# Recurrent stage of a hybrid attention, RWKV-7 and Mamba-2 kernel: Gram products over 64 rows in two row groups, and copies in place of transposes around the triangular inverse

## The chip, the cores and the metric

One Trainium2 chip, one core of it. The kernel is one program on the five engines of that core: TensorE (PE in the profile, with its weight loads apart as PEld), VectorE (DVE), ScalarE (ACT), GpSimd (POOL) and SyncE (SP), which issues DMAs. The metric is the time of one execution on the device in microseconds, lower is better; of several executions the median is given. The profile is that of one further execution, which has its own time.

## The reference, cut to what matters

The kernel computes two layers on 512 latent tokens and 256 context tokens of width 1024, batch 1. Layer 0 has differential attention (4 heads) and a bidirectional RWKV-7 mixer (8 heads of 64) side by side, then an output projection and a ConvFFN. Layer 1 has a Mamba-2 mixer and a ConvFFN. The change touches only the RWKV-7 recurrence of layer 0, which runs forward and backward over the tokens:

```python
def rwkv7_scan(r, decay, k, v, kk, a, state0, reverse):
    def step(s, inp):
        r_t, w_t, k_t, v_t, kk_t, a_t = inp
        sa = jnp.einsum('bhij,bhj->bhi', s, kk_t)
        s = (s * w_t[:, :, None, :] - sa[..., None] * (kk_t * a_t)[:, :, None, :]
             + v_t[..., None] * k_t[:, :, None, :])
        return s, jnp.einsum('bhij,bhj->bhi', s, r_t)

    xs = tuple(jnp.moveaxis(z, 1, 0) for z in (r, decay, k, v, kk, a))
    s, y = lax.scan(step, state0, xs, reverse=reverse)
    return jnp.moveaxis(y, 0, 1), s
...
    for d, reverse, s0 in ((0, False, s0_f), (1, True, s0_b)):
        ...
        y, s = rwkv7_scan(r_h, heads(decay), k_d, v_h, kk, heads(a), s0, reverse)
```

## The kernel before

The scan over single tokens is worked in chunks of 64. The 768 tokens are three groups `gi` of 256, each of four chunks `c`, in two directions `d`: 24 units of direction and chunk, each with 8 heads. Heads stand in pairs, a pair `m` on the 128 partitions: the even head on rows 0 to 63, the odd one on 64 to 127. `HALF` lists the two halves as (`par_`, `own`, `oth`): `own` is the rows of that head, `oth` the other half.

For each 128 tokens and direction `prep` (L654) loads slices of r, k and kk, allocates the tiles `z` ([128, 4 pairs, 2 heads, 128]) and makes the decay and the step size through matmuls with `lora` (L673). `prep2` (L680) takes the running product of the decays (the scan L684) and builds `g1`, the scaled kk and k.

`gram` (L709) makes one unit's Gram products, every pair of tokens of the chunk against each other. VectorE writes `z[own, :, par_]` (scaled kk and r). Rows `oth` of that head's part of `z` are zero, from `G.memset` at L665, so that a matmul over all 128 rows gives the product of one head. The four matmuls of one head fill one PSUM bank `gp` of the pool tag `g` (`gps()`, three banks, used by almost all else here too). ScalarE copies the bank out in three pieces: into `mt` (the matrix to be inverted), into `z[oth]` (which takes the place of the zeros) and into `ar`; GpSimd sets the wrong side of the triangles to zero (L729, L732). Then four transposes on TensorE (L737) and three copies make `kb`. `grams` (L930) calls `gram` for both directions and, after each second chunk, `bonus` (L702).

`invert` (L743) inverts the 32 unit lower triangles of 64x64 that a group has, in 32x32 blocks. Blocks on the diagonal are brought to another layout, `dd`, by VectorE transposes: rows 0 to 31 and 64 to 95 (`B0`) and rows 32 to 63 and 96 to 127 (`B1`) of `mt[:, :, 0:32]` by one 128x1024 transpose (L744), after which the rows of `B1` are overwritten from `mt[B1, :, 32:64]` by two 32x1024 transposes (L746). GpSimd selects the triangle (L747). Thirty steps of substitution follow on VectorE, on `dd` and `dt`. At the end two 128x1024 transposes bring `dd` back as `dt` (L761) and into `mt[:, :, 0:32]` (L762), two 32x1024 transposes bring its `B1` rows into `mt[B1, :, 32:64]` (L764), GpSimd clears `mt[B1, :, 0:32]` (L765), and 32x32 matmuls (L773, L776) with copies behind them (L784) work out the block below the diagonal.

`chain` (L806) carries the state over one chunk in both directions, with matmuls at L827, L836, L843, L851 and L862; `rh` is a ScalarE copy between L827 and L843.

The three inverses are: of group 0 (all of its Grams come first), of group 1 (its Grams stand among the chunks of group 0), and of group 2 (among those of group 1). Beside them `ada_gen` (L938; its loads L947, its matmuls L957) streams 80 loads of 512 KB of `in_ada_w` through three buffers `aws`, with matmuls into one bank `adaps`; it has nothing to do with the recurrence and fills gaps. Within group 2 `att_part` (L975; its matmuls L983) makes a part of the output projection. The order of each engine's instructions comes from a scheduler that goes by priority and by what is ready; `ada_run` raises the priority of its steps.

```python
z = ring("z", [128, 4, 2, 128])
for par_, own, oth in HALF:
    G.memset(z[oth, :, par_, :], 0.0)
...
for par_, own, oth in HALF:
    gp = gps()
    for m in range(4):
        PE.matmul(gp[:, m, :], lhsT=g1[:, m, cl].rearrange("p s t -> p (s t)"),
                  rhs=z[:, m, par_, :], start=True, stop=True)
```

## Time and profile before

| | |
|---|---|
| runs | 2372.32, 2364.98, 2360.39 us |
| median | 2364.98 us |
| the profiled execution's own time | 2373.08 us |
| span of that execution's profile | 2371.4 us |
| TensorE busy | 2218.2 us (94%) |
| VectorE busy | 1380.5 us (58%) |
| ScalarE busy | 1003.0 us (42%) |
| GpSimd busy | 341.2 us (14%) |
| recurrent stage, in the span | about 355 to 782 us |

A row of the page's groups gives line, engine, operation, what is written from what, shape, and the count behind x; then the busy time in us and the mean of one in ns; then the idle time of that engine just before them and what ended most of it. A row of a timeline gives start and duration in us, then the same names, and in square brackets the idle time before it with its releaser. On TensorE a form such as 64*64 behind a matmul is rows by columns of the array. A matmul in float32 appears as two records.

### The profile page before, as it was taken

The numbers are of one execution on the slowest core, as the hardware profiler recorded it, in microseconds if no ns is written. First come the engines' busy times: TensorE is split into PE (matmuls) and PEld (weight loads), VectorE is DVE, ScalarE is ACT, GpSimd is POOL, SyncE is SP. The second block draws the span as 40 slices with busy tenths as digits, with TensorE's granted clock in tenths as the row PEclk, the third lists the DMA queues.
The fourth block names the chain that finished last, engine by engine and source line by source line (L and its number), as shares of the span: only waits on it lengthen the run. The fifth ranks groups of instructions, "written<-read, shape, count | busy, mean of one in ns | idle before, by whom it ended". The sixth has DMA issues, their size and how long they took to land.

```text
span 2371.4 us, 38461 instructions
## 1 busy us (share of the span) xinstructions
PE 2218.2 (94%) x15644; PEld 1984.3 (84%) x15644; DVE 1380.5 (58%) x2513; ACT 1003.0 (42%) x1904; POOL 341.2 (14%) x358
## 2 busy tenths in 40 slices
PE   6999998698879899999999998999999998999998
PEld 5889998476768799999999987888888877888887
DVE  4766737748586653333324468867666766434445
ACT  4655537474733342112212345544444544323233
POOL 1000005342510020000000022223222123000000
PEclk9999989799979999999999999999899999999999
DMA  8111222677455512222222301111111112333332
GB/s 271 44 52 49 89 86 80 211 226 224 133 165 171 156 50 66 63 62 63 63 63 63 98 23 45 45 45 55 53 54 54 36 45 63 107 98 95 95 96 88
DMA packets 302128, 216.09 MB, mean 91 GB/s; under 512 B 8832, under 2 KB 272640, under 8 KB 301952
## 3 DMA queue, kind: packets, MB, share of 16 engines
q1 hardware_dynamic: 301952, 213.64, 29.7%
q8 instruction: 123, 2.02, 0.3%
q14 instruction: 53, 0.43, 0.1%
HBM read 197.36 MB, written 16.25 MB: 90 GB/s over the span
## 4 chain that ended last, share of the span: by engine, by line
PE 78%; DVE 11%; ACT 4%; DMA 3%; issue 2%; POOL 1%; SPq 0%; DVEq 0%; ACTq 0%; POOLq 0%
PE dps L208 41%; PE dps L1428 9%; PE dps L1208 3%; PE dps L1421 3%; DMA aws<-in_ada_w 2%; PE g L724 1%; PE adaps L957 1%; PE aps L983 1%; PE dps L1143 1%; PE tps L517 1%; DVE cv L146 1%; DVE dt L137 1%; DVE nacc L137 1%; DVE dd L137 1%; DVE xw L137 1%
## 5 line engine op out<-in xcount | busy, mean ns | idle before, releaser
L134 ACT ACTIVATE wh<-ws 128x1024 fp32r<-128x1024 f32 x196 | 208.0, 1061 | 603.7 <-PE dps L208 466.5
L208 PE MATMUL dps<-hh,wl 128*128 128x384 f32 (+1 forms) x1368 | 401.0, 352 | 1.3 <-DVE wl L150 1.3
L208 PE MATMUL dps<-hl,wh 128*128 128x384 f32 (+1 forms) x1368 | 400.3, 352 | 0.0
L208 PE MATMUL dps<-hh,wh 128*128 128x384 f32 (+1 forms) x1368 | 398.5, 352 | 1.6 <-ACT vT L134 0.9
L150 DVE TENSOR_TENSOR wl<-ws,wh 128x1024 fp32r<-128x1024 f32 x136 | 166.5, 1224 | 202.7 <-ACT wh L134 190.6
L208 PEld LDWEIGHTS dps<-hh,wh 128*128 128x128 f32 x1368 | 251.3, 190 | 15.9 <-ACT vT L134 1.3
L208 PEld LDWEIGHTS dps<-hh,wl 128*128 128x128 f32 x1368 | 251.3, 189 | 15.1 <-DVE wl L150 1.6
L208 PEld LDWEIGHTS dps<-hl,wh 128*128 128x128 f32 x1368 | 251.3, 189 | 14.0 <-issue 0.3
L1356 POOL TENSOR_TENSOR wl<-ws,wh 128x1024 fp32r<-128x1024 f32 x52 | 125.3, 2410 | 319.9 <-ACT wh L134 282.3
L1428 PE MATMUL dps<-hh,wh 128*128 128x384 f32 (+1 forms) x448 | 147.4, 380 | 14.7 <-DVE sz L146 13.6
L1428 PE MATMUL dps<-hl,wh 128*128 128x384 f32 (+1 forms) x448 | 144.3, 372 | 0.0
L1428 PE MATMUL dps<-hh,wl 128*128 128x384 f32 (+1 forms) x448 | 142.1, 369 | 0.0
L146 DVE SCALAR_TENSOR_TENSOR cv<-dps,cwh,cv 128x511 f32<-128x511 f32 (+3 forms) x176 | 109.6, 623 | 30.9 <-ACT cv L134 28.3
L208 PE MATMUL dps<-al,wh 128*128 128x384 f32 (+1 forms) x384 | 114.8, 352 | 0.0
L208 PE MATMUL dps<-ah,wl 128*128 128x384 f32 (+1 forms) x384 | 114.8, 352 | 0.0
L208 PE MATMUL dps<-ah,wh 128*128 128x384 f32 (+1 forms) x384 | 114.7, 352 | 0.0
L137 DVE TENSOR_TENSOR fg<-fg,dps 128x768 f32<-128x768 f32 (+1 forms) x44 | 36.1, 821 | 129.7 <-PE dps L208 127.1
L1428 PEld LDWEIGHTS dps<-hh,wh 128*128 128x128 f32 x448 | 85.4, 197 | 26.2 <-DVE sz L146 15.1
L146 DVE SCALAR_TENSOR_TENSOR fg<-dps,par,fg 128x511 f32<-128x511 f32 (+1 forms) x132 | 85.1, 658 | 15.9 <-ACT fg L134 13.5
L1428 PEld LDWEIGHTS dps<-hh,wl 128*128 128x128 f32 x448 | 86.8, 198 | 7.5
L1428 PEld LDWEIGHTS dps<-hl,wh 128*128 128x128 f32 x448 | 86.5, 197 | 6.2
L146 DVE SCALAR_TENSOR_TENSOR x<-dps,mod,x 128x256 f32<-128x256 f32 (+1 forms) x56 | 31.9, 594 | 102.0 <-PE dps L208 99.6
(575 smaller groups left out, 4548.2 us busy)
## 6 DMA issues: line engine op xcount, KB each, us to landing
aws<-in_ada_w SPq DMA_DIRECT2D x96, 512.0 KB, 5.2
ws<-in_ffn_w_up SPq DMA_DIRECT2D x88, 512.0 KB, 3.8
ws<-in_ssm_w_in SPq DMA_DIRECT2D x40, 512.0 KB, 3.9
ws<-in_ffn_w_down SPq DMA_DIRECT2D x32, 512.0 KB, 3.6
ws<-in_ev_w_in SPq DMA_DIRECT2D x26, 512.0 KB, 4.0
ws<-in_ssm_w_out SPq DMA_DIRECT2D x16, 512.0 KB, 3.4
ws<-in_ffn_w_down SPq DMA_DIRECT2D x16, 384.0 KB, 3.2
projd<-tsh SPq DMA_DIRECT2D x12, 384.0 KB, 2.6
```

The source lines that it names most:

```text
L134: S.activation(out=o, in_=i, func=func, bias=bias, scale=scale, **kw)
L137: V.tensor_tensor(out=o, in0=x, in1=y, op=op)
L146: V.scalar_tensor_tensor(out=o, in0=x, scalar=s, in1=y, op0=op0, op1=op1)
L150: eng.tensor_tensor(out=lo, in0=src, in1=hi.bitcast(F32), op=ALU.subtract)
L208: PE.matmul(ps[:, po:po + hi - lo], lhsT=w[:, k0 + k, :], rhs=x[:, xk0 + k, lo:hi], start=(first and k == 0 and j == 0), stop=(last and k ...
L517: PE.matmul(po[:, 0:n], lhsT=w[:, kk, :], rhs=xx[:, kk, 0:n], start=(kk == 0 and j == 0), stop=(kk == nk // 128 - 1 and j == 2))
L724: PE.matmul(gp[:, m, :], lhsT=g1[:, m, cl].rearrange("p s t -> p (s t)"), rhs=z[:, m, par_, :], start=True, stop=True)
L957: PE.matmul(ps[32 * g:32 * g + 32, 0:128], lhsT=cs[:, k0 + k, :], rhs=ws[i][:, k, g * 128:(g + 1) * 128], start=(k0 + k == 0), stop=(k0 + ...
L1208: PE.matmul(ps[:, off + lo:off + hi], lhsT=w[:, k, :], rhs=x_[:, lo:hi], start=(k == 0 and j == 0), stop=(k == nk - 1 and j == 2))
L1356: G.tensor_tensor(out=lo, in0=w, in1=hi.bitcast(F32), op=SUB)
L1421: PE.matmul(ps[:, 512 * h:512 * h + 512], lhsT=w[:, k, h * 128:(h + 1) * 128], rhs=x[k], start=(k == 0 and j == 0), stop=(k == 3 and j == 2))
L1428: PE.matmul(ps[:, po:po + hi - lo], lhsT=w[:, k, :], rhs=x[:, k, lo:hi], start=(k == 0 and j == 0), stop=(k == KD - 1 and j == 2))
```

## The change

The change has three parts.

First, the zero fills of `z` go. The Gram matmuls take only the 64 rows of one head, of `g1` as of `z`; the heads of a pair lie on the two halves of the array's rows. Both PSUM banks are taken first, and the loops are turned round, so that the two heads' matmuls alternate. The copies behind them stay as they are.

Second, `lower` copies `mt[B1, :, 32:64]` over `mt[B1, :, 0:32]` on ScalarE, once for chunks 0 to 2 of a group (after chunk 2's Grams) and once for chunk 3. The one 128x1024 transpose at the start of `invert` then finds all diagonal blocks in columns 0 to 31, and the two 32x1024 transposes behind it go.

Third, the two 32x1024 transposes at the end of `invert` become two ScalarE copies of `mt[B1, :, 0:32]` into `mt[B1, :, 32:64]`.

```diff
-                    zs = []
-                    for c in range(2):
-                        z = ring("z", [128, 4, 2, 128])
-                        for par_, own, oth in HALF:
-                            G.memset(z[oth, :, par_, :], 0.0)
-                        zs.append(z)
+                    zs = [ring("z", [128, 4, 2, 128]) for _ in range(2)]
...
+                    gpp = [gps(), gps()]
+                    for m in range(4):
+                        for par_, own, oth in HALF:
+                            PE.matmul(gpp[par_][:, m, :], lhsT=g1[own, m, cl].rearrange("p s t -> p (s t)"),
+                                      rhs=z[own, m, par_, :], start=True, stop=True)
                     for par_, own, oth in HALF:
-                        gp = gps()
-                        for m in range(4):
-                            PE.matmul(gp[:, m, :], lhsT=g1[:, m, cl].rearrange("p s t -> p (s t)"),
-                                      rhs=z[:, m, par_, :], start=True, stop=True)
+                        gp = gpp[par_]
                         act(mt[own, u0:u0 + 4, :], gp[0:64, :, 0:64], AF.Copy)
...
+                def lower(mt, c0, c1):
+                    v = mt.rearrange("p (d u) t -> p d u t", d=2)[:, :, 4 * c0:4 * c1, :]
+                    for i in range(2):
+                        act(v[B1[i], :, :, 0:32], v[B1[i], :, :, 32:64], AF.Copy)
+
                 def invert(mt):
                     V.transpose(out=dd, in_=mt[:, :, 0:32].rearrange("p u t -> p t u"))
-                    for i in range(2):
-                        V.transpose(out=dd[B1[i]], in_=mt[B1[i], :, 32:64].rearrange("p u t -> p t u"))
...
                     for i in range(2):
-                        V.transpose(out=mt[B1[i], :, 32:64].rearrange("p u t -> p t u"), in_=dd[B1[i]])
+                        act(mt[B1[i], :, 32:64], mt[B1[i], :, 0:32], AF.Copy)
                         G.memset(mt[B1[i], :, 0:32], 0.0)
...
                         out[d, c] = gram(d, c, ps[d], mt)
+                    if c in (2, 3):
+                        lower(mt, *((0, 3), (3, 4))[c - 2])
```

Three places show how the scheduler's order moves. Line numbers of the changed kernel differ: the Gram matmul is L719 there, the transposes behind it L734, the ada matmul L959, the bonus copy L702, and L746 is the one 128x1024 transpose.

VectorE at the start of the third inverse, before (`bon` is the bonus copy, `vv` belongs to the chain, `mod` to ada, and the last row is the first step of substitution):

```order
L137 TENSOR_TENSOR vv<-st,wc 64x4x64
L744 STREAM_TRANSPOSE dd<-mt 128x1024
L707 COPY bon<-g 128x8 x2
L746 STREAM_TRANSPOSE dd<-mt 32x1024
L137 TENSOR_TENSOR vv<-st,wc 64x4x64 x2
L746 STREAM_TRANSPOSE dd<-mt 32x1024
L137 TENSOR_TENSOR mod<-adaps,par 128x8
L749 MEMSET dd 128x32
L137 TENSOR_TENSOR dt<-dd 128x30
```

The same place after the change (`bs` is the sum of the two directions' bonuses):

```order
L137 TENSOR_TENSOR vv<-st,wc 64x4x64
L702 COPY bon<-g 128x8 x2
L137 TENSOR_TENSOR bs<-bon 128x8
L746 STREAM_TRANSPOSE dd<-mt 128x1024
L137 TENSOR_TENSOR vv<-st,wc 64x4x64 x2
L749 MEMSET dd 128x32
L137 TENSOR_TENSOR dt<-dd 128x30
```

Two transposes are gone, and the one that is left stands behind the bonus copies, where it stood ahead of them.

VectorE at the end of the third inverse, before (`rsq` belongs to the normalization that runs beside it):

```order
L268 RECIPROCAL rsq<-rsq 128x8
L761 STREAM_TRANSPOSE dt<-dd 128x32x32
L762 STREAM_TRANSPOSE mt<-dd 128x32x32
L764 STREAM_TRANSPOSE mt<-dd 32x32x32 x2
L784 COPY dt<-c 32x512 x2
L137 TENSOR_TENSOR rsq<-rsq 128x8
```

After:

```order
L761 STREAM_TRANSPOSE dt<-dd 128x32x32
L762 STREAM_TRANSPOSE mt<-dd 128x32x32
L268 RECIPROCAL rsq<-rsq 128x8
L137 TENSOR_TENSOR rsq<-rsq 128x8
L150 TENSOR_TENSOR ol<-ow,oh 128x512
L137 TENSOR_TENSOR rsq<-rsq,rsv 128x8
L143 TENSOR_SCALAR rsq<-rsq 128x8
L137 TENSOR_TENSOR rsq<-rsq 128x8
L784 COPY dt<-c 32x512 x2
```

The pair L764 has left VectorE, and small work of the normalization has moved into its place, ahead of the copies of L784.

ScalarE in group 0, between two chunks of the chain, before (`adaev` belongs to ada; the `kb` copies end a Gram):

```order
L134 ACTIVATE kb<-g 128x4x64
L134 ACTIVATE kb<-g 64x4x64 x2
L134 ACTIVATE adaev<-adaps 128x128
L134 ACTIVATE rh<-c 128x256 x2
```

After:

```order
L134 ACTIVATE kb<-g 128x4x64
L134 ACTIVATE kb<-g 64x4x64 x2
L134 ACTIVATE mt<-mt 32x2x12x32 x2
L134 ACTIVATE adaev<-adaps 128x128
L134 ACTIVATE rh<-c 128x256 x2
```

The two copies of `lower` stand behind the Gram's last copies and ahead of the chain's `rh`.

## The prediction

> **What bounds the kernel now.** I read three views: the page's share of the chain that ended last, the same chain followed inside two stretches of the recurrent stage (355 to 520 us, then 520 to 710 us of the span), and the busy time by stretch.
>
> ```profile
> PE 78%; DVE 11%; ACT 4%; DMA 3%; issue 2%; POOL 1%; SPq 0%; DVEq 0%; ACTq 0%; POOLq 0%
> ```
>
> The two stretches:
>
> ```profile
> by line: PE g L724 13.6%; DMA aws<-in_ada_w 13.5%; PE adaps L957 8.2%; issue 6.3%; PE g L673 5.3%; DVE dt L137 5.0%; DVE dd L137 5.0%; DVE g L137 3.7%; DVE sg L684 3.3%; PE g L706 3.2%; PE g L737 2.9%; DMA gd<-gt 2.8%; POOL br L699 2.3%; DV
> by line: DMA aws<-in_ada_w 11.2%; PE adaps L957 7.7%; issue 7.2%; PE g L724 5.6%; PE c L851 4.3%; DVE dd L746 4.2%; DVE dt L137 3.8%; DVE dd L137 3.4%; PE y L862 3.4%; PE g L706 2.4%; DVE z L146 2.3%; ACT z L134 2.2%; PE c L843 2.2%; DVE vv
> ```
>
> Over the whole span the matmuls carry the chain (78%). Inside the recurrent stage the picture is mixed: Gram matmuls (L724) hold 13.6% of the first 165 us and 5.6% of the next 190 us, so 22.4 + 10.6 = 33 us; the wait for the ada weights holds 13.5% and 11.2%, 22.3 + 21.3 = 44 us; the two 32x1024 transposes L746 hold 4.2% of 190 us, 8 us.
>
> ```profile
> 480.00:500.00 20.00, 18.73 (x239) 15.13 (x240) 5.07 (x15) 17.25 (x45) 7.84 (x15) 1.00 0.81 256
> 565.00:600.00 35.00, 28.86 (x520) 21.56 (x520) 32.03 (x68) 22.42 (x54) 11.00 (x17) 0.85 0.69 219
> 592.00:612.00 20.00, 17.96 (x187) 14.95 (x188) 9.53 (x21) 17.61 (x46) 10.23 (x20) 1.00 0.57 177
> 612.00:632.00 20.00, 16.89 (x275) 15.10 (x275) 16.61 (x33) 15.85 (x43) 16.43 (x21) 0.83 0.32 107
> ```
>
> The columns are the busy time of PE, weight loads, VectorE, ScalarE and GpSimd, the granted clock, the DMA share and GB/s. In stretches of Grams (480 to 500, 592 to 612) TensorE and ScalarE are both busy 86 to 94% of the time; at the end of the second inverse (565 to 600) VectorE is, 32.0 of 35 us. So no one engine bounds the stage; what an edit is worth depends on the stretch.
>
> Measured against its own execution: the sum below is made against the profiled run's own 2373.1 us (2.7 of which lies outside the span of 2371.4), and then put on the median of the three runs, 2365.0, which is 8.1 lower. A measurement of this kernel can tell about 0.5%, 11.8 us, from no change.
>
> **Gram matmuls in two row groups.**
>
> ```profile
> 506.08 2.05 PE L724 MATMUL g<-z,g 128*128 128x128 f32 x16
> 507.97 0.60 PE L737 MATMUL g<-cst,g 128*128 128x128 f32 x4
> 763.59 1.15 PE L843 MATMUL c<-rh,mt 64*64 64x64 f32 x32
> 764.75 0.33 PE L851 MATMUL c<-vv,kb 128*64 128x64 f32 x2
> ```
>
> One Gram now is 8 matmuls of 128 rows, two passes each, so 16 records, and the transposes begin 1.89 us after it: 118 ns a record. With 24 Grams that is 45.4 us. The trace has no row-group pair on one set of columns. The nearest it has are tiles on the diagonal (L843, 64 rows by 64 columns, two halves in turn): 32 records from 763.59 to 764.75, 36 ns each. At half of the moving columns 118 ns would be 59; the other factor of nearly two is two tiles at work together. If two row groups do the same, a Gram takes 0.95 us; if not, 1.89 as before.
>
> ```profile
> 464.42 0.41 PE L957 MATMUL adaps<-aws,cs 128*32 128x128 f32 x2
> 464.76 0.24 PE L773 MATMUL c<-dt,mt 32*32 32x32 f32 x2
> 464.93 0.41 PE L957 MATMUL adaps<-aws,cs 128*32 128x128 f32 x2
> ```
>
> This alternation has a pair of 32-column and a pair of 32x32 matmuls. One round takes 0.51 us (464.42 to 464.93), and the work in it about 0.11, 2 x 28 ns by the 128 records of L773 in 3.63 us (quoted below) and about as much for L957; so about 0.4 for two changes of form, 0.2 us each. Each Gram now gets one change more, to the 128-row transposes behind it, and often one ahead. So 1.89 - 0.95 - 0.2 to 0.4 = 0.55 to 0.75 us a Gram, 13 to 18 us of TensorE time over 24. Bounds: 0.95 x 24 = 22.7 saved without any price for the change of form; 0.4 x 24 = 9.6 lost with two changes and no overlap. [...]
>
> ```profile
> L724 PE MATMUL g<-z,g 128*128 128x128 f32 x384 | 58.2, 302 | 12.2 <-POOL z L665 3.3 <-DVE z L137 3.2 <-issue 1.7
> L134 ACT ACTIVATE z<-g 64x512 f32<-64x512 f32 x48 | 28.5, 594 | 0.7
> L134 ACT ACTIVATE kb<-g 64x256 f32<-64x256 f32 x48 | 18.2, 379 | 0.6
> L134 ACT ACTIVATE ar<-g 64x256 f32<-64x256 f32 x48 | 18.1, 377 | 1.1
> L134 ACT ACTIVATE mt<-g 64x256 f32<-64x256 f32 x48 | 18.0, 376 | 7.8 <-PE g L724 6.8
> L134 ACT ACTIVATE kb<-g 128x256 f32<-128x256 f32 x24 | 9.2, 385 | 0.6
> ```
>
> Behind each Gram ScalarE evacuates 2x594 + 2x376 + 2x377 + 2x379 + 385 ns = 3.84 us a Gram (28.5 + 18.2 + 18.1 + 18.0 + 9.2 = 92 us over 24), against 1.89 + 0.53 on TensorE. Where ScalarE runs without a break, a shorter Gram gives nothing.
>
> ```profile
> 483.04 0.38 ACT L134 ACTIVATE ar<-g 64x256 f32<-64x256 f32 x1
> 483.44 1.17 ACT L134 ACTIVATE kb<-g 128x256 f32<-128x256 f32 x3
> 484.86 0.38 ACT L134 ACTIVATE mt<-g 64x256 f32<-64x256 f32 x1 [0.25 <-PE g L724]
> ```
>
> There the second direction's first copy waited 0.25 us for its half Gram, which had begun while the other half's bank was being evacuated. After the change both banks must be free, so its Gram starts behind the `ar` copy (483.42) and has the 1.17 us of `kb` copies to hide in; 0.95 + 0.2 just fits. If it waits, what is queued behind it on TensorE waits too: its transposes, then matmuls of the other chain and of ada. Of the 33 us on the chain I put half into such stretches (ScalarE is at 86 to 88% there); a third (0.65 of 1.89) of the other 16.5 is saved: **-5.5 us**. Bounds 0.95/1.89 of 33, -16.5, and +9.6.
>
> **Start of the inverse.**
>
> ```profile
> 647.18 0.17 DVE L707 COPY bon<-g 128x8 f32<-128x8 f32 x1 [1.51 <-PE g L706]
> 647.36 2.00 DVE L746 STREAM_TRANSPOSE dd<-mt 32x1024 f32<-32x1024 f32 x1
> ...
> 653.68 0.17 DVE L137 TENSOR_TENSOR dt<-dd 128x30 f32<-128x30 f32 x1 [1.22 <-issue]
> ```
>
> In the third inverse the two transposes (the second is left out above) stand between the second bonus copy (647.18) and the first substitution step (653.68). After the change the one 128x1024 transpose stands alone there.
>
> ```profile
> L747 POOL TENSOR_SCALAR_AFFINE_SELECT dd<-dd 128x1024 f32<-128x1024 f32 x3 | 3.8, 1268 | 2.1 <-DVE dd L746 2.1
> ```
>
> It starts behind the copy at 647.35 (the order puts it there), ends at 649.3, the triangle's select takes 1.27, and the step starts at about 650.7: -3.0.
>
> ```profile
> 535.89 1.99 DVE dd L746
> ```
>
> In the second inverse the pair is a piece of the chain too (this is the first of it), again -3.0.
>
> ```profile
> 431.37 1.23 DVE L684 TENSOR_TENSOR_SCAN sg<-rmask,sg 128x512 f32<-128x512 bf16 x1
> ```
>
> In the first, the step at 432.56 came behind this scan, which the change leaves: 0 to -1, I take -0.5. Together **-6.5 us** (bounds -4 to -11.8, the whole group of six at 1966 ns).
>
> **End of the inverse.**
>
> ```profile
> 689.36 1.94 DVE L762 STREAM_TRANSPOSE mt<-dd 128x1024 f32<-128x1024 f32 x1
> 691.33 3.84 DVE L764 STREAM_TRANSPOSE mt<-dd 32x1024 f32<-32x1024 f32 x2
> ```
>
> TensorE at that place:
>
> ```profile
> 689.60 3.63 PE L773 MATMUL c<-dt,mt 32*32 32x32 f32 x128 [10.10 <-DVE dt L761]
> ...
> 695.95 3.62 PE L776 MATMUL c<-mt,dt 32*32 32x32 f32 x126 [2.29 <-DVE dt L784]
> ```
>
> The pair L764 (3.84 us) leaves VectorE; two copies of 32x1024 on ScalarE take its place behind L762, which ends at 691.3. They wait for L762, and behind them in ScalarE's order stand the `dt` copies that L776 needs.
>
> ```profile
> L134 ACT ACTIVATE wh<-ws 128x1024 fp32r<-128x1024 f32 x196 | 208.0, 1061 | 603.7 <-PE dps L208 466.5
> ```
>
> I price one by this 128x1024 row, 1.06 us, since a copy's time goes with what lies along a row (64x256 takes 376 ns, 128x256 385). So `mt` is complete at 693.5, the first `dt` copy on ScalarE ends at 694.1, VectorE's earlier, and L776 starts at 694.2, not 695.95: -1.8. In the second inverse VectorE is the busy engine (565 to 600): 3.84 less, 0.9 given back to the copies, about -3. In the first, TensorE interleaves L773 with ada matmuls beside it: -1.5. Together **-6.3 us** (bounds 0 to -11.5).
>
> **What ScalarE gets.** Six copies of 1.06 us at the ends, counted above on their path; and `lower`, whose two copies of 768 and two of 256 elements a row go at 0.84 and 0.38 by the nearest rows: 2.4 us an inverse, 7.3 in all. `lower` reads what ScalarE itself wrote, so it waits for nobody, but it stands ahead of the `rh` copy, for which the chain's L843 waits. Their cover is ScalarE's idle time; in the unbroken stretches there is none. I take half, **+3.5** (bounds 0 and 7.3 + 6.4 = +13.7).
>
> **Zero fills.**
>
> ```profile
> L665 POOL MEMSET z<- 64x512 f32 x48 | 25.4, 530 | 314.3 <-DMA gd<-gt 298.6 <-PE y L836 13.3 <-PE g L706 0.3
> ```
>
> GpSimd loses 25.4 us of memsets. L724 waited 3.3 us for them by its group row, and behind them GpSimd's selects come sooner: **-2** (0 to -5).
>
> Sum: -5.5 - 6.5 - 6.3 + 3.5 - 2 = -16.8; I take -16, since a stall that goes leaves the ada loads next in line. 2373.1 - 16 = 2357 for a run like the profiled one, **2349** on the median.
>
> **The rivals.**
> - *ScalarE is the bound* where the Grams stand. For it: 3.84 us of evacuation a Gram against 2.4 on TensorE. Against: L724 is the largest line of the chain there. Then the Gram term is 0 and `lower` counts in full: -6.5 - 6.3 + 7.3 - 1 = -6.5, 2358. [...] Chance 0.16.
> - *The ada loads are the bound.* Three buffers of 512 KB, refilled in order; their wait is 44 us of the chain, and the DMA share is 0.81 from 480 to 500. From 425 to 600 us a gain then only lengthens the next wait for a load. Left are the last inverse (-4.8), a third of the Gram term (-1.8) and half of the zero fills: -7.5, 2357. Chance 0.12.
> - *Row groups do not overlap.* Then a Gram takes 1.89 + 0.3, and the second direction's Gram, which now waits for both banks, ends 1.0 us behind the `kb` copies: 12 of 24 times about 0.8, +9.6, half of it in stretches where ScalarE waits: +5 in place of -5.5: -6, 2359; all of it, 2363. Chance 0.08.
> - *The clock falls* (the other side). In the Gram stretches 480 to 500 and 592 to 612 the granted clock is 1.00 with TensorE busy 94 and 90%, and in 612 to 632, at 84%, it is 0.83. A Gram of half the length leaves TensorE more idle. A 4 us window at half clock instead of full costs about 2 us where TensorE sets the pace; 8 such windows more than now (32 us) eat the 16 us, the point from which it decides; 14 of them, nearly all of the three Gram stretches quoted (60 us), give +12, 2377. Against it: each new gap is under 1 us. Chance 0.08.
> - *More than forecast*: the Gram term at -12 and VectorE's relief in full, -28, 2337. Chance 0.08.
>
> **How the numbers follow.** The forecast, -9 to -24, has 0.48 (2341 to 2356). The range 2334 to 2368 takes in it, the first three rivals with the spread of single runs (2360 to 2372), and part of the last; it leaves out the clock and the far end. Faster by over 0.5% (below 2353): three quarters of the forecast, the last rival, and some of the first two, 0.50. Slower by over 0.5% (above 2377): most of the clock case, 0.07. The rest 0.43.
>
> **What would show it.** Grams right: rows of 64*128 form in place of L724, 16 in about 1.0 us, and less of that line on the chain; wrong: 16 in 1.9. Start: the first `dt` step about 3.4 us behind the second bonus copy. End: L776 some 6.6 us behind the start of L761, not 8.4. ScalarE: `lower` rows in idle time, or ahead of a late `rh`. Wrong as a whole if the ada wait grows by what the others lose, or if the granted clock of the Gram stretches drops below 1.00.

## The result, and the profile after

The changed kernel takes 2398.76 us, median of four runs (2393.53 to 2405.17), against 2364.72 us before (four runs, 2360.39 to 2372.32): the ratio is 1.014, 95% interval 1.0119 to 1.016. It is 34 us slower where 16 us faster was forecast, and outside the stated range. A second measurement of it on another occasion, beside the kernel before, gave 1.0129 (1.008 to 1.0177).

The chain that ended last, on the page of the changed kernel, by engine:

```profile
PE 81%; DVE 8%; ACT 5%; DMA 3%; issue 2%; POOL 1%; SPq 0%; DVEq 0%; ACTq 0%
```

TensorE's share of the chain has gone from 78 to 81% and VectorE's from 11 to 8%: what VectorE lost on the path, TensorE took, and more. The Gram line itself (L719) now holds 10.8% of the chain from 355 to 520 us and 11.6% from 520 to 710, together 40 us; the old one held 33. Where TensorE's time went stands in the busy time by stretch, in the same four stretches as before (PE, weight loads, VectorE, ScalarE, GpSimd, then granted clock, DMA share, GB/s):

```profile
480.00:500.00 20.00, 18.76 (x193) 13.61 (x183) 3.18 (x12) 12.69 (x31) 7.88 (x15) 0.84 0.76 242
565.00:600.00 35.00, 26.95 (x407) 18.21 (x403) 28.43 (x102) 11.61 (x28) 4.69 (x6) 0.70 0.68 217
592.00:612.00 20.00, 20.00 (x330) 13.93 (x331) 11.18 (x17) 8.59 (x16) 4.17 (x7) 0.50 0.45 133
612.00:632.00 20.00, 19.96 (x118) 16.50 (x116) 4.15 (x11) 12.13 (x29) 8.92 (x16) 0.50 0.31 88
```

The clock was 1.00, 0.85, 1.00 and 0.83 there; it is now 0.84, 0.70, 0.50 and 0.50. From 592 to 632 us TensorE is busy without a gap, at half clock, for 40 us. Stretches at fixed times hold different work in the two runs, so I also summed, over all 4 us windows from 355 to 815 us, TensorE's busy time times 2(1 - clock), which is its busy time at half clock: 56 us before, 157 us after. This is an estimate: it takes TensorE's busy time in a window as spread evenly over it, and the clock as either 1.00 or 0.50, which are the only values in these two traces. The two profiled executions took 2373.08 and 2405.17 us.

The two runs part at the last Gram ahead of the end of an inverse. At the second inverse, before:

```profile
573.68 2.08 PE L724 MATMUL g<-z,g 128*128 128x128 f32 x8
576.70 1.52 PE L724 MATMUL g<-z,g 128*128 128x128 f32 x8
578.26 1.26 PE L773 MATMUL c<-dt,mt 32*32 32x32 f32 x68
```

After:

```profile
587.17 1.65 PE L719 MATMUL g<-z,g 64*128 64x128 f32 x6
589.15 1.65 PE L719 MATMUL g<-z,g 64*128 64x128 f32 x8
594.71 2.02 PE L773 MATMUL c<-dt,mt 32*32 32x32 f32 x68
631.53 6.26 PE L668 MATMUL g<-wa,lora 128*128 128x256 f32 x16
```

Both Grams start at half clock (0.50), which has held from 567 us before and from 579 us after. Behind the 128-row Gram full clock is back at 577.5 us (1.00 from 577.5 to 590), just ahead of the 32x32 matmuls at the inverse's end, and their first 68 records take 1.26 us. Behind the 64-row Gram it is not; the same 68 take 2.02 us, and full clock returns only at 636.7 us (0.50 from 579 to 636.7), within the 128-row matmuls L668. From the start of L761 to the end of the last L776 it takes 19.3 us there, against 12.7 before. The first inverse shows the same, 22.0 against 15.8 us. In the third the clock is at half (0.50) in both runs, and it takes 12.8 against 12.0.

The new Gram rows, from the groups of the recurrent stage and from TensorE's timeline at full clock:

```profile
L719 PE MATMUL g<-z,g 64*128 64x128 f32 x384 | 59.1, 346 | 9.4 <-ACT ar L134 3.3 <-DVE z L137 1.9 <-ACT ta L134 1.6
```

```profile
374.55 1.92 PE L719 MATMUL g<-z,g 64*128 64x128 f32 x16 [0.56 <-ACT ar L134]
376.41 0.66 PE L734 MATMUL g<-cst,g 128*128 128x128 f32 x4
```

This Gram takes 1.86 us (374.55 to 376.41), as long as with 128 rows (1.89), so its two row groups hardly worked at the same time. The program's order on TensorE is the likely reason: of the 24 Grams the scheduler put ten as four matmuls of one head and then four of the other, seven as 3+3+1+1, two in between, and only five in turn, as the code is written. One head's operands and bank are ready first, and its matmuls go first.

Two timings of the third inverse, VectorE and then TensorE:

```profile
682.30 0.17 DVE L137 TENSOR_TENSOR bs<-bon 128x8 f32<-128x8 f32 x1 [1.71 <-PE g L283]
682.39 1.94 DVE L746 STREAM_TRANSPOSE dd<-mt 128x1024 f32<-128x1024 f32 x1
684.26 1.76 DVE L137 TENSOR_TENSOR vv<-st,wc 64x256 f32<-64x256 f32 x2
686.12 0.09 DVE L749 MEMSET dd<- 128x32 f32 x1
686.22 0.66 DVE L137 TENSOR_TENSOR dt<-dd 128x30 f32<-128x30 f32 x2
```

```profile
719.44 3.63 PE L773 MATMUL c<-dt,mt 32*32 32x32 f32 x128 [6.93 <-DVE dt L761]
...
726.62 3.62 PE L776 MATMUL c<-mt,dt 32*32 32x32 f32 x126
```

The first substitution step comes 3.8 us behind the start of the first transpose (682.39 to 686.22), against 10.0 before (643.65 to 653.68). The row of 126 records of L776 begins 9.2 us behind the start of L761 (717.43), against 8.4 before: the end gained nothing here.

### The profile page after: what moved, and what is told of

The parts are those of the page before. It is cut to its first block, busy times and chain, and to the rows that moved or that the text cites. A ratio compares the mean times of both kernels' runs of the same rounds, so it can differ in the third digit from the quotient of the medians.

```text
span 2403.5 us, 38385 instructions
## 1 busy us (share of the span) xinstructions
PE 2255.2 (94%) x15644; PEld 2007.1 (84%) x15644; DVE 1362.2 (57%) x2501; ACT 1016.3 (42%) x1922; POOL 309.8 (13%) x310
## 3 DMA queue, kind: packets, MB, share of 16 engines
q8 instruction: 123, 2.02, 0.3%
## 4 chain that ended last, share of the span: by engine, by line
PE 81%; DVE 8%; ACT 5%; DMA 3%; issue 2%; POOL 1%; SPq 0%; DVEq 0%; ACTq 0%
PE dps L208 41%; PE dps L1430 9%; PE dps L1210 3%; PE dps L1423 3%; PE adaps L959 2%; PE g L719 2%; DMA aws<-in_ada_w 1%; PE dps L1145 1%; PE tps L517 1%; PE aps L985 1%; DVE cv L146 1%; PE c L851 1%; PE g L668 1%; DVE nacc L137 1%; PE s L484 1%
## 5 line engine op out<-in xcount | busy, mean ns | idle before, releaser
L150 DVE TENSOR_TENSOR wl<-ws,wh 128x1024 fp32r<-128x1024 f32 x136 | 166.4, 1224 | 202.9 <-ACT wh L134 190.9
L208 PEld LDWEIGHTS dps<-hl,wh 128*128 128x128 f32 x1368 | 251.4, 189 | 13.9 <-issue 0.3
L959 PE MATMUL adaps<-aws,cs 128*32 128x128 f32 x1280 | 73.5, 333 | 24.9 <-DMA aws<-in_ada_w 17.4
L146 DVE SCALAR_TENSOR_TENSOR fg<-dps,par,fg 128x511 f32<-128x511 f32 (+1 forms) x132 | 85.1, 658 | 16.3 <-ACT fg L134 13.9
```

The source lines that it names most:

```text
L146: V.scalar_tensor_tensor(out=o, in0=x, scalar=s, in1=y, op0=op0, op1=op1)
L150: eng.tensor_tensor(out=lo, in0=src, in1=hi.bitcast(F32), op=ALU.subtract)
L208: PE.matmul(ps[:, po:po + hi - lo], lhsT=w[:, k0 + k, :], rhs=x[:, xk0 + k, lo:hi], start=(first and k == 0 and j == 0), stop=(last and k ...
L959: PE.matmul(ps[32 * g:32 * g + 32, 0:128], lhsT=cs[:, k0 + k, :], rhs=ws[i][:, k, g * 128:(g + 1) * 128], start=(k0 + k == 0), stop=(k0 + ...
```

## The experiments

Ratios are to the kernel before, timed on the same chip beside each. Theory A: the 64-row Grams keep the granted clock down. B: the ScalarE copies hold up `rh` and the evacuation. C: the two banks taken at once, and the alternation, hold up TensorE. D and E concern what the copies are worth.

**The copies alone.** The Gram part of the change undone:

```diff
-                    gpp = [gps(), gps()]
...
+                    for par_, own, oth in HALF:
+                        gp = gps()
+                        for m in range(4):
+                            PE.matmul(gp[:, m, :], lhsT=g1[:, m, cl].rearrange("p s t -> p (s t)"),
+                                      rhs=z[:, m, par_, :], start=True, stop=True)
```

> Gram products as before (128 rows, zero fills, one bank at a time); of the change only the ScalarE copies for the four transposes. Theory A (the 64-row Gram matmuls lower the granted clock, and that is the whole loss): the copies give their own -6 to -14, so 2351 to 2359, and the granted clock by stretch is that of before, 1.00 in the Gram stretches. Theory B (the copies on ScalarE stand ahead of rh and of the Grams' evacuation, and that is the loss): 2385 or more. Theory C (two banks taken at once and the alternation of row groups hold up TensorE): as A, about 2355.

Measured 2368.02 us, 1.000 (0.9985 to 1.0015); TensorE's time at half clock 66 us. B falls. But A's forecast of -6 to -14 falls with it: the copies are worth nothing.

**The Gram part alone**, all seven transposes as before (the first two hunks of the change and no more).

> Only the Gram part of the change (64 rows, row groups in turn, two banks first, no zero fills); all seven transposes as before. Theory A: 2395 to 2412, the full loss plus what the copies gave, with half clock over long parts of 455 to 640 us. Theory B: 2355 to 2365. Theory C: as A in time, but the clock falls only where TensorE waits.

Measured 2387.95 us, 1.0085 (1.0055 to 1.0116); 128 us at half clock. The Gram part loses by itself; the sum "full loss plus what the copies gave" was too high.

**The Gram part with the loop order of before.**

```diff
                     for par_, own, oth in HALF:
                         gp = gps()
                         for m in range(4):
-                            PE.matmul(gp[:, m, :], lhsT=g1[:, m, cl].rearrange("p s t -> p (s t)"),
-                                      rhs=z[:, m, par_, :], start=True, stop=True)
+                            PE.matmul(gp[:, m, :], lhsT=g1[own, m, cl].rearrange("p s t -> p (s t)"),
+                                      rhs=z[own, m, par_, :], start=True, stop=True)
```

> 64 rows and no zero fills, but the loop order and the single bank of before: four matmuls of one row group, then four of the other. Transposes as before. Theory A: still slow, 2390 to 2412, since each matmul still fills half of the rows. Theory C (alternation and the two banks): back at 2355 to 2368. A Gram's 16 records take 1.86 to 1.9 us at full clock if row groups did not overlap in turn either; longer than that if they had overlapped.

Measured 2390.43 us, 1.0091 (1.006 to 1.0122); 145 us at half clock. No better, so C is not needed for the loss.

**The new loop order with 128 rows.**

```diff
+                    gpp = [gps(), gps()]
+                    for m in range(4):
+                        for par_, own, oth in HALF:
+                            PE.matmul(gpp[par_][:, m, :], lhsT=g1[:, m, cl].rearrange("p s t -> p (s t)"),
+                                      rhs=z[:, m, par_, :], start=True, stop=True)
```

> The kernel before with one edit: both PSUM banks of a Gram are taken first and the two heads' matmuls are written in turn; still 128 rows with zero fills, and all seven transposes. Theory A (the 64-row Gram keeps the clock down): 2360 to 2375 with the clock of before. Theory C (the two banks and the order hold up TensorE): 2385 to 2392, as the Gram part alone gave.

Measured 2370.12 us, 1.0025 (1.0004 to 1.0046); 65 us at half clock. Two banks at once cost 1 to 11 us, 6 by the middle of the interval; the time at half clock stays near the 56 us of before.

**TensorE by itself, without idle time.** The rest of the kernel is left out; streams of one form follow each other. The two 64-row streams differ in `both`:

```python
def rows64(n, both):
    for i in range(n):
        h = R[i % 2 if both else 0]
        PE.matmul(banks[2 + (i % 2 if both else 0)][:, i // 2 % 4, :], lhsT=w(i)[h], rhs=r(i)[h], start=True, stop=True)
```

> The rest of the kernel is left out: only streams of matmuls on TensorE, each behind a stretch of 128-row ones. Theory A: 128-row and 64-row streams both run at about 118 ns a record at full clock (no gain from two row groups), and in the 64-row streams, alternating or not, the granted clock goes to 0.50 though TensorE never idles; likewise in the streams of 64x64, 128x64 and 128x32 tiles where too little of the array is at work. The mix of 8 64-row and 4 full matmuls ends lower than the mix of 12 full ones. Rival: the clock stays at 1.00 in every stream, since TensorE is busy throughout; then the loss is due to idle gaps, and a 64-row stream that overlaps shows about 60 ns a record.

Three streams, from its timeline (L145 is 128 rows; L150 64 rows, first in turn, then one row group only):

```profile
10.88 46.29 PE L145 MATMUL bk<-x 128*128 128x128 f32 x400 [10.88 <-DMA x<-in_xT]
57.10 22.60 PE L150 MATMUL bk<-x 64*128 64x128 f32 x400
...
106.63 44.93 PE L150 MATMUL bk<-x 64*128 64x128 f32 x400
...
340.06 1.16 PE L150 MATMUL bk<-x 64*128 64x128 f32 x16
341.16 1.16 PE L145 MATMUL bk<-x 128*128 128x128 f32 x8
342.25 1.16 PE L150 MATMUL bk<-x 64*128 64x128 f32 x16
```

116 ns a record with 128 rows, 56 in turn, 112 in one row group. So in turn the two row groups did work at the same time: 56 ns against 112. Sixteen records in turn take 1.10 us up to the 128-row matmuls behind them (340.06 to 341.16), 0.2 above 16 x 56 ns: as much for the change of form as the prediction had taken. The clock was 1.00 in the streams of 64 rows in turn (57 to 80 us), of one row group (107 to 151), of 64x64 tiles (178 to 208) and of 32 columns (291 to 313), and 0.994 over the whole run. Theory A, as I had put it, falls: here half-filled rows did not lower the clock, in 44 us without a stop. What was left was that they might not raise it again.

**The return of the clock.** The rest of the kernel is left out; each stream stands behind a gap of 7 us, at the end of which the clock is at half (0.50). In the alternation each of the two matmuls always goes to one place of the array (its first 32 columns; its first 64 rows and columns).

> The rest of the kernel is left out. Streams of one form each, every one behind a gap of some 8 us in which TensorE idles, so that it starts at half clock. Theory A in the form the first bench left it (64-row streams stay at full clock when they start there): the 128-row stream returns to full clock within a few us; streams of 64 rows in blocks of four, 64x64, 128x32, and above all the alternation of 32-column and 64x64 matmuls return later or not at all. Of the three mixes (8 Gram matmuls, 4 full, 8 pairs in alternation), that with 128-row Grams returns first. Rival: every stream returns after the same few us.

Two of its stretches, 128-row matmuls and the alternation of 32-column with 64x64 matmuls:

```profile
47.00:82.00 35.00, 34.60 (x297) 34.60 (x298) 0.35 (x1) 0.00 (x0) 0.95 0.00 1
241.00:299.00 58.00, 57.63 (x239) 27.67 (x239) 0.31 (x1) 0.00 (x0) 0.50 0.00 1
```

Every stream of one form came back to full clock: 128 rows after 2.9 us, 64 rows in turn after 5.1 and in blocks after 6.0, 64x64 after 5.6, 32 columns after 4.1. That is later than 128 rows, as I expected, but by a few us only and from one stretch each. In the clock's own records in the traces of the kernels before and after, each half-clock stretch but the last, which the end of the trace cuts, lasts 3.41 us or a whole multiple of it; so differences of this size may come from where in such a step a stream begins. In blocks of four the 300 records took 24 us at a mean clock of 0.87 (133 to 157 us), by estimate 70 ns a record at full clock, between the 56 in turn and the 112 of one row group. The alternation did not come back in 58 us (0.50 throughout), though the profile shows TensorE busy for 57.6 of them. By estimate most of that is changes of form, counted as busy: a pair took 0.96 us, and its four records, at the 28 and 29 ns of the first bench's streams (800 of 32 columns in 22.04 us, 1000 of 64x64 in 29.38), come to 0.23 at half clock. The kernel has similar work behind an inverse: ada matmuls of 32 columns and 32x32 matmuls in turn, with a change of form each time (0.51 us a round at 1.00 before, 0.81 at 0.50 after).

The last three stretches of this run, not shown, were six rounds each of 8 Gram matmuls, 4 full ones and 8 alternating pairs. With 128-row Grams full clock was back 3.4 us after the start. The other two began at full clock, behind a gap of only 2.3 us, and fell to half within 2 us. With blocks of four and four it stayed there for 27 us, in turn for 3.4.

**Grams within such an alternation.** The rest of the kernel is left out; five rounds of 8 Gram matmuls (`g`) and 8 alternating pairs, behind a gap.

```python
def mix(n):
    for i in range(n):
        cols32(1)
        diag64(1)
...
for b, g in ((0, full), (6, blk64), (6, alt64), (6, full), (6, blk64), (6, alt64)):
    gap(banks[b])
    full(1)
    for i in range(5):
        g(8)
        mix(8)
```

> The rest of the kernel is left out. Six stretches, each behind a gap in which TensorE idles: five rounds of 8 Gram matmuls and 8 pairs of a 32-column and a 64x64 matmul. The Grams are of 128 rows, of 64 rows in blocks of four and four, of 64 rows in turn, and then the three again. If what counts is the share of the array at work: with 128 rows full clock in the first or second round, with blocks of four late or never, with turns in between. If only TensorE's being busy counts: all three the same.

Its six stretches, in order 128 rows, blocks of four and four, in turn, and the three again (PE, weight loads, VectorE, GpSimd, clock):

```profile
47.00:82.00 35.00, 34.80 (x232) 23.78 (x232) 0.15 (x1) 0.00 (x0) 0.91 0.00 1
91.00:145.00 54.00, 54.00 (x242) 32.72 (x241) 0.16 (x1) 0.00 (x0) 0.50 0.00 0
153.00:183.00 30.00, 30.00 (x240) 18.52 (x240) 0.10 (x1) 0.00 (x0) 0.96 0.00 1
190.00:225.00 35.00, 34.89 (x241) 23.73 (x241) 0.75 (x2) 0.00 (x0) 0.96 0.00 1
232.00:287.00 55.00, 54.56 (x242) 33.10 (x242) 0.71 (x3) 0.00 (x0) 0.50 0.00 1
293.00:339.00 46.00, 42.78 (x242) 25.02 (x242) 2.63 (x4) 0.00 (x0) 0.64 0.11 46
```

With 128 rows the clock was back in the first round, both times (0.91 and 0.96 over the stretch). With blocks of four it was not back in five rounds, either time (0.50), and the five rounds took 54 us, not 35. In turn it was back at once the first time (0.96), in the fourth round the second (0.64). Length alone does not explain it: the 16 records at half clock took about 3.7 us with 128 rows, 3.1 in blocks and 2.1 in turn, so the ones in turn were the shortest. Blocks and turns do the same multiplications; by these times, what differs is how much of the array works at once. Over both runs full clock came back within 6 us, of the start or of the fall, in three of three stretches with 128 rows, in two of three in turn and in none of three with blocks. That the share of the array counts is the reading that fits best; no run varied it in steps. Streams of one form had brought the clock back in 2.9 to 6.0 us; a TensorE that the profile shows busy without a break stayed at 0.50 for 54 us with blocks among the alternation, and one busy for 57.6 of 58 us with the alternation alone. Here being busy by the profile was not enough.

**Full matmuls added to the Gram part.** The four transposes of each Gram done three times over:

```diff
-                    for m in range(4):
+                    for m in (0, 1, 2, 3) * 3:
                         PE.transpose(tp[:, m, :], g1[:, m, cl].rearrange("p s t -> p (s t)"), ident)
```

> The Gram part alone (64 rows), with its four 128-row transposes done three times over: 8 full matmuls more a Gram, about 0.95 us at full clock and 23 us of TensorE in all, to no use. Theory A (too little of the array at work keeps the clock at half): half clock gets shorter in 455 to 640 us, and the time is no worse than 2388, perhaps 2370 to 2385, in spite of the added work. If the clock has nothing to do with it: 2388 plus 10 to 20, 2398 to 2408, clock as in the Gram part alone.

Measured 2391.89 us, 1.0114 (1.0082 to 1.0146); time at half clock 81 us, down from 128. So with full-array work added the clock was up for longer in the kernel too. The 23 us of added work (an estimate at full clock) bought back 47 us at half clock, so 23 us of TensorE; the time is between the two forecasts and not told apart from the Gram part alone.

**Grams held in turn**, first with the copies and then without: the eight matmuls as one unit for the scheduler.

```diff
+                    with tc.tile_critical():
+                        for m in range(4):
+                            for par_, own, oth in HALF:
```

> The changed kernel, with the eight Gram matmuls held in the order in which they are written, so that all 24 Grams issue the two heads' matmuls in turn (the scheduler let 5 of 24 do so and put ten as four and four). A Gram's 16 records should take about 0.95 to 1.1 us at full clock, as in the bench, not 1.86. Theory A with the array's fill as what counts (two row groups at once fill it as 128 rows do): TensorE's time at half clock goes back from 157 us towards 56 to 90 and the time to 2350 to 2375. If a Gram of half the length is too short to bring the clock back: half-clock time stays at 130 to 160 us, 2380 to 2400.

> As alt_crit, but with all seven transposes on VectorE as before, so that only the Gram part differs from the kernel before. Theory A as there: 2350 to 2372; with a Gram too short: 2375 to 2390. Against alt_crit it says what the copies are worth once the row groups work in turn; by the run with the copies alone (ratio 1.000), 0 plus or minus 5.

Measured 2454.92 us, 1.0388 (1.0355 to 1.0421), and 2443.99 us, 1.0337 (1.0295 to 1.0379); 152 and 162 us at half clock. The first kernel's timeline and the second's Gram row:

```profile
375.97 1.16 PE L720 MATMUL g<-z,g 64*128 64x128 f32 x16 [1.15 <-DVE z L146]
377.22 0.54 PE L735 MATMUL g<-cst,g 128*128 128x128 f32 x3
```

```profile
L720 PE MATMUL g<-z,g 64*128 64x128 f32 x384 | 40.1, 368 | 56.0 <-DMA aws<-in_ada_w 19.5 <-POOL ar L727 12.6 <-DMA slkk<-projd 8.4
```

The Gram shown now takes 1.25 us up to its transposes, but in the second kernel TensorE idled 56 us ahead of the Grams, 12.2 in the kernel before, most of it for ada loads, for GpSimd and for other loads: that nothing passes the unit while it waits is the likely reading. This way of holding the order costs more than the whole question. On the clock the two runs disagree: through the ends of the first two inverses it was at 1.00 in the first and at 0.50 in the second.

**Grams in turn by their operands.** One VectorE instruction writes the last column of both halves, so that they are ready together:

```diff
-                        tt(z[own, :, par_, 64:128], rv[own, :, cs_], wx[own, :, cl, 1:65], MUL)
+                        tt(z[own, :, par_, 64:127], rv[own, :, cl * 64:cl * 64 + 63], wx[own, :, cl, 1:64], MUL)
+                    tt(z[:, :, :, 127], rv[:, :, cl * 64 + 63].unsqueeze(2).to_broadcast([128, 4, 2]),
+                       wx[:, :, cl, 64].unsqueeze(2).to_broadcast([128, 4, 2]), MUL)
```

> The Gram part alone (64 rows, transposes as before), with the last column of both heads' halves of z written by one VectorE instruction, so that the two heads' operands come ready together: 14 of 24 Grams now go wholly or mostly in turn, 9 still as four and four for want of the second bank (with the Gram part alone: 5 and 11). If what is lost comes from blocks of four that fill half of the array: TensorE's time at half clock falls from 128 us to 70 to 110 and the time from 2388 to 2365 to 2382. If Grams in turn are too short to bring the clock back, no gain or a loss: 2385 to 2400.

Measured 2393.31 us, 1.013 (1.0088 to 1.0171); 137 us at half clock. More Grams in turn bring neither time nor clock back; the forecast of 70 to 110 us failed. In the second stretch in turn of the bench, with Grams of half the length, the clock came back only in the fourth round; that nine still stand as four and four may be part of it too. It was not told apart.

**Which copies pay.** `lower` alone on the kernel before; then the copies at the end alone; then the Gram part with `lower`.

```diff
+                    if c in (2, 3):
+                        lower(mt, *((0, 3), (3, 4))[c - 2])
...
-                    for i in range(2):
-                        V.transpose(out=dd[B1[i]], in_=mt[B1[i], :, 32:64].rearrange("p u t -> p t u"))
```

```diff
-                        V.transpose(out=mt[B1[i], :, 32:64].rearrange("p u t -> p t u"), in_=dd[B1[i]])
+                        act(mt[B1[i], :, 32:64], mt[B1[i], :, 0:32], AF.Copy)
```

> The kernel before with the copies of lower on ScalarE and one transpose at the start of the inverse; the four transposes at its end stay. Theory D (the start is the part that pays: the first step comes 6 us sooner in three inverses, and the copies ahead of rh give back 2 to 3 us each): 2355 to 2362, ratio 0.996 to 0.999. Theory E (what is saved at the start is waited for elsewhere, since TensorE's own work sets the pace between the inverses): 1.000.

> The kernel before with only the two transposes at the end of the inverse turned into ScalarE copies. In the run with both parts the last L776 came 12.8 to 15.7 us behind the start of L761, as before (12.0 to 15.8), so no gain: ratio 0.999 to 1.003. By the forecast's term of -6.3 us: 0.9973.

> The changed kernel with the transposes of before at the end of the inverse: Gram part and lower. If lower is what adds to the loss there (ScalarE is the engine that evacuates the Grams): 1.012 to 1.016. If it is the end copies, or chance between runs: 1.005 to 1.011.

Measured 1.0001 (0.9988 to 1.0013), 1.0007 (0.9991 to 1.0024) and 1.0079 (1.0051 to 1.0107). Neither part pays on the kernel before, as theory E had it; `lower` does not add to the loss of the Gram part. VectorE at the third inverse with `lower` alone:

```profile
647.08 0.17 DVE L707 COPY bon<-g 128x8 f32<-128x8 f32 x1 [2.35 <-PE g L706]
647.27 1.99 DVE L749 STREAM_TRANSPOSE dd<-mt 128x1024 f32<-128x1024 f32 x1
649.19 1.77 DVE L137 TENSOR_TENSOR vv<-st,wc 64x256 f32<-64x256 f32 x2
...
651.12 0.61 DVE L137 TENSOR_TENSOR dt<-dd 128x30 f32<-128x30 f32 x1
```

The step is 3.9 us behind the transpose, not 10.0. But the transpose itself now waits for the bonus copy ahead of it (TensorE's L706), which it used to precede: from that copy the step was 6.5 us away (647.18 to 653.68) and is 4.0, so 2.5 us are saved, not 6. In this run the second inverse's substitution took 35.4 us against 32.8, and from the end of one inverse to the start of the next went 62.3 and 58.4 us, against 56.6 and 55.9. That gives the rest back. In profiles of single runs, of a kernel whose own times spread over 18 us (2356 to 2374), this is an indication and no more.

**Full matmuls in idle time of the kernel before**, 40 of them, not read, late in the third substitution.

```diff
+                        if warm and k in (20, 28):
+                            wm = fps()
+                            wv = dd[:, k - 4:k, :].rearrange("p a b -> p (a b)")
+                            for i in range(20):
+                                PE.matmul(wm[:, i % 4, :], lhsT=wv, rhs=wv, start=True, stop=True)
```

> The kernel before, with 40 full 128-row matmuls to no use (their results are not read) at two late steps of the third inverse's substitution, where TensorE idles or runs at half clock. If dense work of the full array is what brings the clock back: L773 and L776 of the third inverse at full clock, 1.2 us each in place of 3.6, the stage behind them sooner, and the time lower by 3 to 8 us. If the clock there is set otherwise: 0 to +5 us.

Measured 2363.32 us, 0.9995 (0.9978 to 1.0013). L773 took 2.59 us in place of 3.63, but the clock fell to half at 684 us, while L773 still ran, 3.4 us behind the added work (its last row ends at 680.7), and L776 still took 3.62. The forecast of -3 to -8 is not borne out: that the full-array work ended too early to carry the clock through the end of the inverse is my reading; no run told it apart.

**Full matmuls behind the inverses of the changed kernel**, 24 at each (not read), with the changed kernel once more beside it.

> The changed kernel with 24 full 128-row matmuls to no use (results not read) behind the last copies of each inverse: 48 records, 5.6 us at full clock and up to 11 at half, in each of three places. If dense full-array work brings the clock back there, and its late return is the loss: half clock ends within about 8 us behind the second inverse in place of some 26, TensorE's time at half clock falls from 157 to 70 to 110 us, and the time is 10 to 25 us below that of the changed kernel, in spite of the added work. If not: 15 to 25 us above it.

> The changed kernel once more, beside after_warm on the same chip: 2393 to 2405, ratio about 1.014, with 130 to 160 us of TensorE's time at half clock.

The added lines, at the end of `invert`:

```diff
+                    wm = fps()
+                    wv = mt[:, 16:18, :].rearrange("p u t -> p (u t)")
+                    for i in range(24):
+                        PE.matmul(wm[:, i % 4, :], lhsT=wv, rhs=wv, start=True, stop=True)
```

Measured 2409.98 us, 1.0191 (1.0164 to 1.0217), and 2399.24 us, 1.0129 (1.008 to 1.0177); 135 and 147 us at half clock. TensorE behind the second inverse, with the added matmuls:

```profile
615.55 2.67 PE L719 MATMUL g<-z,g 64*128 64x128 f32 x14
618.14 7.23 PE L788 MATMUL c<-mt 128*128 128x128 f32 x48
625.30 0.48 PE L719 MATMUL g<-z,g 64*128 64x128 f32 x2
```

The clock came back within them, by the windows at about 621 us (0.50 up to 619, 0.68 from 619 to 623, then 1.00), in place of 637 in the changed kernel, 6 us after the last L776 (615.6), where it had taken 27 (610.2). But TensorE's time at half clock fell only to 135 us, not to 70 to 110, and the time went up by 11 us, not down. The half-clock work ahead of that point, from about 587 us, was untouched, and the 48 records took 7.2 us here alone. So the clock rose within full-array work here too (0.50 to 1.00 at about 621 us); that the time can be bought back at a profit is not shown.

TensorE's busy time at half clock, 355 to 815 us, by the profiled run of each kernel:

| kernel | Gram | us at half clock | ratio |
|---|---|---|---|
| before | 128 rows | 56 | 1 |
| lower only / end copies only / both | 128 rows | 64 / 57 / 66 | 1.0001 / 1.0007 / 1.000 |
| new loop order | 128 rows | 65 | 1.0025 |
| Gram part / with lower | 64 rows | 128 / 138 | 1.0085 / 1.0079 |
| loop order of before | 64 rows | 145 | 1.0091 |
| partly in turn | 64 rows | 137 | 1.013 |
| whole change, twice | 64 rows | 157, 147 | 1.014, 1.0129 |
| held in turn, with copies / without | 64 rows | 152 / 162 | 1.0388 / 1.0337 |
| Gram part and triple transposes | 64 rows | 81 | 1.0114 |
| before, with matmuls in the third substitution | 128 rows | 56 | 0.9995 |
| whole change, with matmuls behind the inverses | 64 rows | 135 | 1.0191 |

Every kernel with 128-row Grams has 56 to 66 us, every one with 64 rows and no added work 128 to 162.

The ends of the inverses say the same, place by place. In all six kernels with 128 rows the granted clock was 0.93 to 1.00 from the first L773 to the last L776 of the first and of the second inverse. From the start of L761 to the end of that L776 it took 15.7 to 17.3 us in the first and 12.3 to 13.9 in the second. In the eight with 64 rows whose order was not held, the clock there was 0.50 to 0.63, and it took 19.8 to 22.9 and 16.8 to 19.5 us. In the third inverse, with clocks of 0.50 to 0.60, both kinds took 10.7 to 12.9.

## Why the prediction was wrong

**Gram matmuls: the step that failed.** "If two row groups do the same, a Gram takes 0.95 us" held in the bench (0.90 and 0.2 for the change of form) and not for the program, where most Grams did not go in turn and one took 1.86 us: the loops were written in turn, and the scheduler issued them mostly in blocks. The prediction had this as a rival, "row groups do not overlap", but took it for a question about the chip. It was one about the order, which could be read before the run. The term of -5.5, with bounds of -16.5 and +9.6, measured +20 us (13 to 27) for the Gram part alone, zero fills included. The rival's time of 2359 to 2363 was too low as well, for the next reason. The 0.2 us a change came out by luck as much as by its working: the 28 ns a record in it were read from L773 in the third inverse, where the clock was 0.50, and set against an alternation at 1.00.

**The clock: the rival that happened.** It had a chance of 0.08 and a price of +12. The sum itself had no term for the clock. The rival named the right sign, a clock below 1.00 in the Gram stretches, but its mechanism was wrong: it is not that shorter Grams leave TensorE more idle, since from 592 to 632 us it is busy without a gap (39.96 of 40 us, clock 0.50). Late in the second substitution TensorE had little to do (busy 2.2 of 4 us from 563 to 567 before, 0.8 of 3.5 from 575.5 to 579 after), and there the clock fell to half. In the kernel before it came back within the last 128-row Gram ahead of the inverse's end at the first two inverses (at 461.4 and 577.5 us), zeros and all, and the alternation of small tiles behind it then ran at 1.00. Within the last 64-row Gram there it did not (at the first inverse it fell in it, at 455.8 us), nor within the alternation, and it came back late (at 483.1 and 636.7 us). That makes 101 us more of TensorE's time at half clock, by estimate 50 us of work, against 34 us more in all. About 13 of the 34 stand at the ends of the first two inverses (6.2 and 6.5 us), where the clock is seen to differ. That the rest is the clock too is argued from this sum and from the Gram part losing by itself; no run took the clock back without adding work. The price was small because it counted windows that fall, one by one, and not a state that lasts, in the changed kernel for 27 us at the first inverse and 58 at the second.

**Start of the inverse**, -6.5. The step does come sooner. With `lower` alone it came 4.0 us behind the second bonus copy of the third inverse (forecast 3.4), which saves 2.5 us (forecast 3.0). In the changed kernel it came 5.8 us behind that copy (680.43 to 686.22), since there the sum of the bonuses, which waits for TensorE, stands between. The size on the path was wrong: with the copies of `lower` it measured 0 +/- 3 us for all three inverses together.

**End of the inverse**, -6.3. Measured +0.0007 of 2366, so +2 us, -2 to +6. With the end copies alone the last L776 of the third inverse ended 10.7 us behind L761's start, against 12.0 before, by that run's trace: 1.3 us gained, forecast 1.8. At the other two inverses nothing was gained (16.2 and 13.7 us against 15.8 and 12.7). The term's second part failed, the -3 at the second inverse because VectorE is busy there (32.0 of 35 us).

**What ScalarE gets**, +3.5, and the **zero fills**, -2: not measured apart. `lower` and the start together came to nothing.

The copies were argued from places where they shorten one engine's row, and added up as if each place were on one path. In this stage the engines take turns, and the 1 to 3 us that a place gained did not show in the time; that the next wait absorbed them is the likely reading, from traces of single runs.

What stays open: why the whole change costs some 0.5% more than its Gram part, by the middles of the intervals, although the copies alone cost nothing. The clock behind the second inverse returned at about 608 us with `lower` and the transposes at the end, and at 637 and 632 in the two runs of the whole change. In the bench, too, it came back at once in one stretch in turn and in the fourth round of the other, so a different order may be all of it; that was only argued. Whether the share of the array at work raises the clock, and how large a share for how long, was not found; nor was it told apart from how much of its busy time TensorE spends on changes of form. No kernel here beats the one before.

## What to carry to other kernels

Zero rows in a matmul can be worth their work: ahead of a stretch of small tiles in alternation, the granted clock came back here within a block of full 128-row matmuls (at 577.5 us, the second inverse) and with 64 rows only at 636.7, so look at the clock by 4 us windows, and at the work within which it rises, before making dense work smaller. Two row groups overlapped in full here where their matmuls were issued in turn (56 ns a record in the bench), while 16 records of a Gram in the changed kernel, where most were not, took 1.86 us; read that order after the scheduler, not in the loops. A saving of 2 to 3 us in a row of one engine counts only if the next wait behind it is known to end sooner.

## What the runs showed of the hardware that was not expected

In the first bench two row groups in turn ran at 56 ns a record, against 116 for 128 rows and 112 for one group alone, and at full clock the change from 64-row to 128-row matmuls cost 0.2 us (1.10 us up to them, less 16 x 56 ns). In the second, TensorE was busy by the profile for 57.6 of 58 us of the alternation and stayed at 0.50; in the third, for 54 of 54 us with blocks among it. The clock's own records in the traces of the kernels before and after know only 1.00 and 0.50, and each stretch of either, but the last of a trace, lasted 3.41 us or a whole multiple of it. Once at full clock it stayed there (1.00) through 44 us of one 64-row group.
